# Fused decoder step: the block sums of the first MLP matrix formed in DRAM by copies on SyncE's queue and adding transfers on GpSimd's, beside the z and gate stages, in place of VectorE additions in the MLP

## The chip, the cores and the metric

The kernel runs on one core of a Trainium2 chip. Its engines each work through their own list of instructions in order: TensorE (PE, with weight loads shown apart as PEld), VectorE (DVE), ScalarE (ACT), GpSimd (POOL) and SyncE (SP). Transfers are issued by SP and POOL (and a few by ACT) and are carried by 16 DMA engines. Engines wait for each other, and for transfers, by semaphores.

The metric is the device time of one execution, in microseconds. Lower is better.

## The reference

One step of one layer over 576 tokens: 512 of a new sequence and 8 times 8 of running ones. An RWKV-7 branch and a differential attention branch read the same normalised input, are merged by gates, and a squared-ReLU MLP and a last norm follow. In one line each, in float32:

```python
xn = rmsnorm(x, g_mix);  P = xn @ w_in                      # 1024 x 5376
Pr = P[..., :RWKV_COLS];  Pr = Pr + (Pprev - Pr) * mu_shift # token shift, "z" columns
o_a, S = rwkv7_branch(Pr, S0, lp)                           # per-token state recurrence
o_b = rmsnorm(attend(q, k, v, lam), subln_g) * (1.0 - lam_init)
m = gate_a * (o_a @ w_br_a) + gate_b * (o_b @ w_br_b)       # gates: sigmoid of P's last 2048 columns
x = x + m @ w_out
hn = rmsnorm(x, g_ffn)
x = x + jnp.square(jax.nn.relu(hn @ w_up)) @ w_down         # 1024 x 4096, 4096 x 1024
y = rmsnorm(x, g_final)
```

The states, the new keys and values and the last normalised row are outputs too.

## The kernel before

**Precision.** A float32 product is formed from halves: each operand is written as hi + lo in the fast fp32r format, and three matmuls (hi x hi, hi x lo, lo x hi) make one product. A weight tile therefore costs ACT one instruction (hi, a copy into fp32r) and DVE one (lo, the rest).

**Weights.** `load` brings a row of a weight matrix (128 output columns by all inputs) in pieces of 4 x 128 rows, 256 KB each, over SP's queue into a ring named raw with three buffers. `stream` splits the pieces and yields once per matmul, so that its matmuls can be dealt out between other work; `dense` runs one to its end.

**Stages.** (1) q, k and v and the attention, to about 180 us. Beside it and the next stage run the streams that fill PE's idle time: `shifted`, fourteen rows of the z columns, and then sixteen rows of gates. (2) Four RWKV chains, one per pair of heads (`rwkv` and `chain`), to about 505 us, with the w_brb products as further filler. In each of them `rwkv` normalises the keys: the column sums pn come from PE, POOL raises them to the power -1/2 (nr, line 760) and spreads them over 64 columns (nb, line 763), and PE transposes nb (pk, line 76). POOL also clears state tiles (ST, line 818, and TT, lines 923 and 924), multiplies masks (vm), and stores results of the attention and the chains to DRAM (ob_d, out_Sp, out_Ss). `rpow` puts the same power on POOL for the group norms (var, line 243). (3) w_bra and w_out, to about 604 us. (4) The MLP, and (5) the last norm.

**The MLP.** `up_pair` forms two rows of 128 hidden columns at once by Strassen's scheme in Winograd's form: with the weights cut in four blocks A11, A12, A21, A22 (two rows of columns by two halves of the inputs) and the tokens in two halves, seven products of 12 matmuls replace eight. Four of the seven left operands are sums of blocks:

S1 = A21 + A22, S2 = S1 - A11, S3 = A11 - A21, S4 = A12 - S2.

The tokens' counterparts (t1 to t4) are made once, while w_out is evaluated. A pair loads its two rows of w_up, 512 KB each (line 1188), into a ring of three; DVE forms S1 to S4 in four additions of 128 x 512 (lines 1204, 1205, 1209, 1210, all issued by the helper at line 61); then each operand is split in hi and lo. There are sixteen pairs. `down` multiplies by w_down between the pairs.

**What sets the order.** Instructions are put in order ahead of time by a scheduler that goes by priorities. Loads have FEED plus 1000 times the number of their job, so they go out in the order of their use, as soon as a buffer of the ring is free; filler matmuls have FILL plus the same. `issue_after` says that something is not to be ordered ahead of a given instruction.

Of the kernel before, what the change touches and what calls it, by code (L numbers as in the profile page):

```python
# [8 lines left out]
F32 = mybir.dt.float32  # L9
F32R = mybir.dt.float32r  # L10
I32 = mybir.dt.int32
AF = mybir.ActivationFunctionType
# [3 lines left out]
P = 128  # L16
# [3 lines left out]
NB = 8  # L20
# [5 lines left out]
DFF = 4096  # L26
# [15 lines left out]
def tile_hybrid_step(ctx, tc, xT, xsT, ktab, vtab, s0T, ptab, w_in, vecs, w2a2, g2, lamv,  # L42
                     w_bra, w_brb, w_out, w_up, w_down, cst, bias_p, bias_s,
                     yT, kTo, vTo, Sp, Ss, sh):
    nc = tc.nc
# [9 lines left out]
    ring = {"job": 0}  # L55

    def act(out, in_, func=AF.Copy, **kw):
        ring["act"] = AE.activation(out=out, in_=in_, func=func, **kw)  # L58

    def tt(out, a, b, op, eng=None):  # L60
        ins = (eng or VE).tensor_tensor(out=out, in0=a, in1=b, op=op)  # L61
# [50 lines left out]
    c = const.tile([P, C_END], F32, name="cst_sb")  # L112
# [29 lines left out]
    def load(src, kt, name):  # L142

        job = ring["job"] = ring["job"] + 1
        n = min(kt, ring["piece"])
        raws = []
        with prio(FEED + 1000 * job):
            for k0 in range(0, kt, n):
                raw = ring["pool"].tile([P, n, P], F32, tag="raw", name=f"raw_{name}_{k0}", bufs=3)
                ring["dma"] = nc.sync.dma_start(out=raw, in_=src[:, k0:k0 + n])  # L150
                raws.append(raw)
        return job, raws

    def stream(src, kt, xh, xl, spans, evac, name, raws=None, together=False, banks=None,
# [108 lines left out]
    oa_d = tc.dram_tile([HB, P, NT], F32, name="oa_d")  # L263
    ob_d = tc.dram_tile([HB, P, NT], F32, name="ob_d")
    gt_d = tc.dram_tile([2 * KT, P, NT], F32, name="gt_d")

    zp = pool("zp", stack=ph1)
    zw = pool("zw", 2, stack=ph1)
# [2 lines left out]
    with tc.tile_pool(name="xin", bufs=2, reuse_waits="tile") as xin:  # L271
# [470 lines left out]
    def rwkv(hp):  # L742
# [3 lines left out]
        r, k, vv = Pt[hp], Pt[4 + hp], Pt[8 + hp]  # L746

        def tmp(tag, bufs=1):
            return rt.tile([P, NT], F32, tag="T", name=f"{tag}_{hp}", bufs=6)


        sq = tmp("sq")
        act(sq, k, AF.Square, scale=v(V_KK + hp))
# [101 lines left out]
            act(KBt[:, c0:c0 + cn].rearrange("p c a t -> p (c a t)"), pK[:, :cn * P])  # L855


        s0 = rt.tile([P, NB, 64], F32, tag="s0", name=f"s0_{hp}")
        nc.sync.dma_start(out=s0, in_=s0T[hp])
        (fill if hp == 3 else take)(8)  # L860
        pI = bank(f"pI{hp}")
        for b in range(NB):
# [265 lines left out]
    for i, d in enumerate((0, 4, 1, 5, 2, 6, 3, 7)):  # L1128
        xr = wt_.tile([P, NT], F32, tag="xr", name=f"xr{d}")
        with prio(FEED + 1000 * (ring["job"] + 1) - 1):  # L1130
            nc.sync.dma_start(out=xr, in_=xT[:, d])
        hf = hfs[d] = wt_.tile([P, NT], F32, tag="hf", name=f"hf{d}", bufs=3)
        k = d % 4

        def ev(ps, t0, n, d=d, k=k, xr=xr, hf=hf):
            x, h = ya[:, d, t0:t0 + n], hf[:, t0:t0 + n]
            tt(x, ps, xr[:, t0:t0 + n], ADD)
            act(h, x, scale=v(V_GF + d))
            if d < 4:
                if t0 == 0:  # L1140
                    put("b11", k, h)
                else:
                    t1 = wt_.tile([P, 288], F32, tag="t", name=f"t1_{k}", bufs=4)
                    tt(t1, h, hf[:, :288], SUB)
                    hfs["t1", k] = t1
                    put("t1", k, t1)
            elif t0:
                for n, x, y in (("t2", h, hfs["t1", k]), ("t3", h, hfs[k][:, 288:])):
                    t = hfs[n] = wt_.tile([P, 288], F32, tag="t", name=f"{n}_{k}", bufs=4)
                    tt(t, x, y, SUB)  # L1150
                    put(n, k, t)
                put("b22", k, h)
            else:
                put("b21", k, h)
                t4 = wt_.tile([P, 288], F32, tag="t", name=f"t4_{k}", bufs=4)
                tt(t4, h, hfs["t2"], SUB)
                put("t4", k, t4)
        dense(w_out[d], KT, mh, ml, HALF[::1 if d < 4 else -1], ev, f"wo{d}")

        for j, (t0, n) in enumerate(HALF):  # L1160
            o = acc[:, t0:t0 + n]
            if i == 0:
# [17 lines left out]
    def up_pair(f1):  # L1180
# [2 lines left out]
        for f in (f1, f2):  # L1183
            qs[f] = hq_pool.tile([P, 2, NT], F32R, tag="q", name=f"q{f}")
        with prio(FEED + 1000 * (ring["job"] + 1)):
            rows = [sp_.tile([P, 2, 4, P], F32, tag="raw", name=f"a{f}", bufs=3) for f in (f1, f2)]
            for r, f in zip(rows, (f1, f2)):
                nc.sync.dma_start(out=r.rearrange("p i k w -> p (i k) w"), in_=w_up[f])
        (a11, a12), (a21, a22) = ([r[:, i] for i in range(2)] for r in rows)
        s12, s34 = (sp_.tile([P, 2, 4, P], F32, tag="s", name=f"s{i}_{f1}", bufs=2) for i in (12, 34))  # L1190

        def halve(x, two, after):

            pl = sp_ if two else ring["pool"]
            shape = [P, 2, 4, P] if two else [P, 4, P]
            hi, lo = (pl.tile(shape, F32R, tag=t + "2" * two, name=f"{t}{after}_{f1}", bufs=3)
                      for t in ("hi", "lo"))
            with prio(FEED + 1000 * (ring["job"] + after) + 100):
                act(hi, x)
                tt(lo, x, f32(hi), SUB)  # L1200
            return [(hi[:, i], lo[:, i]) for i in range(2)] if two else (hi, lo)

        with prio(FEED + 1000 * (ring["job"] + 1) + 90):
            tt(s12[:, 0], a21, a22, ADD)
            tt(s12[:, 1], s12[:, 0], a11, SUB)
        S1, S2 = halve(s12, True, 1)
        A11, A12 = halve(rows[0], True, 2)
# [297 lines left out]
```

## Time and profile before

| | us |
|---|---|
| time, median of 2 (999.0 to 1000.22) | 999.61 |
| profiled execution, span | 1004.0 |
| PE busy | 975.5 |
| DVE busy | 689.5 |
| ACT busy | 497.3 |
| POOL busy | 88.3 |

The profiled execution is one run under the profiler, 4.4 us longer than the median of the runs without it. Its times count from the start of its span. Busy time of an engine is the sum over its instructions; a matmul's end is modelled, so a busy PE is not PE at its peak. In a group's row, the number behind the last bar is the idle time of the engine just before the group's instructions, and what ended it. A wait's row names the waiting engine and tile, the releaser, and the time in all, how often, and the longest. The clock in a row of a stretch is the mean clock granted to TensorE, 1.00 being full speed.

### The profile page before, as it was taken

How to read it: one execution, taken by the hardware profiler on the slowest of the kernel's cores; microseconds unless marked ns; L12 is line 12 of the kernel's file. 1: busy time of each engine (PE TensorE's matmuls, PEld its weight loads, DVE VectorE, ACT ScalarE, POOL GpSimd, SP SyncE). 2: the span in 40 equal slices, each digit the busy share in tenths (PEclk: the TensorE clock that was granted, in tenths of full speed). 3: DMA queues.
4: the chain of work that ended last, by engine and by line, in shares of the span. 5: the costliest groups of instructions: out<-in, count | busy, mean ns of one | idle time of the engine just before them, and what ended most of it. 6: DMA issues, size and time to landing. Idle time of an engine off the chain costs nothing.

```text
span 1004.0 us, 24422 instructions
## 1 busy us (share of the span) xinstructions
PE 975.5 (97%) x10012; PEld 919.9 (92%) x10012; DVE 689.5 (69%) x1459; ACT 497.3 (50%) x1094; POOL 88.3 (9%) x171
## 2 busy tenths in 40 slices
PE   8999999899999999999999999999999999999996
PEld 8999998898887878888889999999999999999996
DVE  6698666774946669445588798966666666666744
ACT  6576555354435344443344666644444444444732
POOL 2511001301010340000300000000000000000001
PEclk9999999999989989999999999999999999999998
DMA  7312673121111225222377642222222222221402
GB/s 265 142 66 88 204 221 120 54 64 45 43 47 57 69 87 171 80 70 102 106 215 237 195 152 74 95 85 95 85 85 95 84 85 85 85 84 44 128 10 95
DMA packets 50833, 105.75 MB, mean 105 GB/s; under 512 B 6066, under 2 KB 8114, under 8 KB 50594
## 3 DMA queue, kind: packets, MB, share of 16 engines
q1 hardware_dynamic: 47442, 96.95, 30.2%
q0 software_dynamic: 1648, 5.35, 1.4%
q8 instruction: 79, 1.29, 0.5%
q10 hardware_dynamic: 1632, 1.89, 0.5%
q14 instruction: 32, 0.26, 0.1%
HBM read 89.38 MB, written 14.78 MB: 104 GB/s over the span
## 4 chain that ended last, share of the span: by engine, by line
PE 86%; DVE 6%; ACT 3%; DMA 2%; issue 2%; POOL 1%; SPq 0%; DVEq 0%; POOLq 0%; ACTq 0%
PE ps_dn L72 21%; PE ps_g L72 9%; PE ps_z L72 8%; PE ua L1224 5%; PE ux L1224 5%; PE ps_wo L72 4%; PE uc L1224 3%; PE ud L1224 3%; PE ub L1224 3%; PE ps_k L72 2%; PE ps_brb L72 2%; PE pch L72 2%; PE ps_q L72 2%; PE ps_v L72 2%; PE pA L72 2%
## 5 line engine op out<-in xcount | busy, mean ns | idle before, releaser
L72 PE MATMUL ps_dn<-q,hi_dn 128*128 128x288 f32 x768 | 154.7, 296 | 0.0
L72 PEld LDWEIGHTS ps_dn<-q,hi_dn 128*128 128x128 f32 x768 | 122.8, 188 | 1.5
L72 PE MATMUL ps_dn<-q,lo_dn 128*128 128x288 f32 x384 | 113.2, 295 | 0.0
L72 PE MATMUL ps_g<-xl,hi_g 128*128 128x288 f32 x256 | 80.2, 313 | 0.0
L72 PE MATMUL ps_g<-xh,lo_g 128*128 128x288 f32 x256 | 79.3, 310 | 0.0
L72 PE MATMUL ps_g<-xh,hi_g 128*128 128x288 f32 x256 | 79.2, 310 | 0.0
L72 PEld LDWEIGHTS ps_dn<-q,lo_dn 128*128 128x128 f32 x384 | 72.1, 188 | 0.0
L72 PE MATMUL ps_z<-xh,lo_z 128*128 128x288 f32 (+1 forms) x224 | 69.6, 311 | 0.0
L72 PE MATMUL ps_z<-xh,hi_z 128*128 128x288 f32 (+1 forms) x224 | 68.3, 305 | 0.0
L72 PE MATMUL ps_z<-xl,hi_z 128*128 128x288 f32 (+1 forms) x224 | 67.6, 302 | 0.0
L61 DVE TENSOR_TENSOR ya<-ya,ps_dn 128x288 f32<-128x288 f32 x96 | 43.4, 453 | 29.3 <-PE ps_dn L72 29.3
L58 ACT ACTIVATE hi_dn<-raw_dn 128x512 fp32r<-128x512 f32 x48 | 30.1, 628 | 57.0 <-PE ps_dn L72 57.0
L1224 PE MATMUL ua<-h_b,hi 128*128 128x288 f32 x256 | 53.2, 298 | 0.0
L1224 PE MATMUL ux<-h_t,hi 128*128 128x288 f32 x256 | 52.3, 296 | 0.0
L58 ACT ACTIVATE c<-c 128x288 f32<-128x288 f32 x112 | 48.4, 439 | 7.5 <-DVE c L61 5.8
L72 PEld LDWEIGHTS ps_g<-xh,hi_g 128*128 128x128 f32 x256 | 49.0, 191 | 2.9 <-issue 1.6
L72 PEld LDWEIGHTS ps_g<-xl,hi_g 128*128 128x128 f32 x256 | 49.0, 191 | 1.9
L72 PEld LDWEIGHTS ps_g<-xh,lo_g 128*128 128x128 f32 x256 | 49.1, 192 | 1.4
L58 ACT ACTIVATE hi<-a 128x1024 fp32r<-128x1024 f32 (+1 forms) x32 | 27.1, 846 | 42.0 <-PE ps_dn L72 34.3
L72 PE MATMUL ps_dn<-q,w 128*128 128x320 f32 (+1 forms) x336 | 46.4, 298 | 0.0
L61 DVE TENSOR_TENSOR lo<-s,hi 128x1024 fp32r<-128x1024 f32 x32 | 39.2, 1225 | 10.2 <-ACT hi L58 10.0
L72 PEld LDWEIGHTS ps_dn<-q,w 128*128 128x128 f32 x336 | 45.3, 190 | 0.1
(395 smaller groups left out, 2801.7 us busy)
## 6 DMA issues: line engine op xcount, KB each, us to landing
a<-in_w_up_dram SPq DMA_DIRECT2D x32, 512.0 KB, 3.3
raw_dn<-in_w_down_dram SPq DMA_DIRECT2D x64, 256.0 KB, 2.9
raw_g<-in_w_in_dram SPq DMA_DIRECT2D x32, 256.0 KB, 3.2
raw_z<-in_w_in_dram SPq DMA_DIRECT2D x28, 256.0 KB, 3.0
gt_d<-gg SPq DMA_DIRECT2D x16, 288.0 KB, 2.5
g<-gt_d SPq DMA_DIRECT2D x16, 288.0 KB, 3.7
kp<-in_ktab_dram SPq DMA_DIRECT2D x16, 256.0 KB, 4.0
vp<-in_vtab_dram SPq DMA_DIRECT2D x16, 256.0 KB, 3.7
```

What stands on the lines that cost most here:

```text
L58: ring["act"] = AE.activation(out=out, in_=in_, func=func, **kw)
L61: ins = (eng or VE).tensor_tensor(out=out, in0=a, in1=b, op=op)
L72: ring["mm"] = PE.matmul(out=out, lhsT=lhsT, rhs=rhs, start=start, stop=stop)
L1224: ring["mm"] = PE.matmul(out=ps[:, :288], lhsT=l[:, k], rhs=hb[blk][:, h, k], start=start and i == 0, stop=i == 11, skip_group_check=skip)
```

## The change

The sums S1 to S4 are no longer made by DVE in the MLP. They are made in DRAM, in a new tensor us_d (16 pairs x 128 partitions x 4 sums x 512), while the z and gate streams run:

- Each sum is one copy of a 256 KB block from w_up to us_d, and one adding transfer, which adds another block to what lies there. The copies are issued by SP; the adding transfers by POOL. There are 64 of each, four per pair.
- `block_sums` is a generator that makes one copy at each step. `load` advances it behind each weight piece of the jobs from the thirteenth on, from the first z row, so a copy stands behind each of the first 64 pieces.
- An adding transfer is put into POOL's order six copies after its own copy, and waits for the landing of that newest copy (`sync_after`). The last six come behind the last copies.
- The second and the fourth sum of a pair add the first and the second, which lie in us_d, so their adding transfer waits for the landing of the one before.

Only additions are used, so two of the sums come out with the other sign: us_d holds A21 + A22, A11 + A21 + A22, A11 + A21 and A12 + A11 + A21 + A22, for the second row taken as negative. t1, t2 and t4 change sign to match, and the second row's ReLU has a scale of -1. `up_pair` now loads S1 and S2 (512 KB), the first row (512 KB), S3 and S4 (512 KB) and A22 (256 KB); the three large tiles share a ring of five, where there had been one of three for the rows and one of two for the sums. In `rwkv` the load of the state s0 stands earlier in the code.

```diff
@@ load
                 ring["dma"] = nc.sync.dma_start(out=raw, in_=src[:, k0:k0 + n])
                 raws.append(raw)
+                if job > 12:
+                    with tc.issue_after(ring["dma"].ins):
+                        next(sums_, None)
@@ new
+    us_d = tc.dram_tile([DFF // 256, P, 4, 4 * P], F32, name="us_d")
+    def sync_after(dma, dep):
+        tc.add_manual_dep(dma.ins, dep.ins.name, mybir.DependencyInfo(
+            mybir.DependencyClass.Sync, mybir.DependencyReason.DATA), reason="pace")
+    def block_sums(n, lag):
+        blk = w_up.rearrange("(g o) p (i k) w -> o i p g (k w)", o=2, i=2)
+        dst = us_d.rearrange("g p s c -> s p g c")
+        a11, a12, a21, a22 = (blk[o, i] for o in range(2) for i in range(2))
+        late = []
+        for g in range(0, DFF // 256, n):
+            at = slice(g, g + n)
+            moves = [(s, src, add) for s, src, add in (
+                (0, a21, a22), (2, a11, a21), (1, a11, dst[0]), (3, a12, dst[1]))]
+            for s, src, add in moves:
+                copy = nc.sync.dma_start(out=dst[s][:, at], in_=src[:, at])
+                late.append((s, add, at))
+                if len(late) > lag:
+                    s, add, at_ = late.pop(0)
+                    with prio(FEED):
+                        dma = nc.gpsimd.dma_start(out=dst[s][:, at_], in_=add[:, at_], accum_op=ADD)
+                    sync_after(dma, copy)
+                yield
+        for s, add, at_ in late:
+            with prio(FEED):
+                nc.gpsimd.dma_start(out=dst[s][:, at_], in_=add[:, at_], accum_op=ADD)
+            yield
+    sums_ = block_sums(1, 6)
...
@@ tokens' blocks
-                    tt(t1, h, hf[:, :288], SUB)
+                    tt(t1, hf[:, :288], h, SUB)
...
+                    if n == "t2":
+                        stt(t, h, -1.0, hfs["t1", k], MUL, SUB)
...
-                tt(t4, h, hfs["t2"], SUB)
+                stt(t4, hfs["t2"], -1.0, h, MUL, SUB)
@@ up_pair
-            rows = [sp_.tile([P, 2, 4, P], F32, tag="raw", name=f"a{f}", bufs=3) for f in (f1, f2)]
-            for r, f in zip(rows, (f1, f2)):
-                nc.sync.dma_start(out=r.rearrange("p i k w -> p (i k) w"), in_=w_up[f])
-        (a11, a12), (a21, a22) = ([r[:, i] for i in range(2)] for r in rows)
-        s12, s34 = (sp_.tile([P, 2, 4, P], F32, tag="s", name=f"s{i}_{f1}", bufs=2) for i in (12, 34))
+            s12, a1, s34 = (sp_.tile([P, 2, 4, P], F32, tag="raw", name=f"{n}{f1}", bufs=5)
+                            for n in ("s12", "a1", "s34"))
+            a22 = ring["pool"].tile([P, 4, P], F32, tag="raw", name=f"a22{f1}", bufs=3)
+            flat = lambda t: t.rearrange("p i k w -> p (i k w)")
+            nc.sync.dma_start(out=flat(s12), in_=us_d[f1 // 2, :, 0:2].rearrange("p s c -> p (s c)"))
+            nc.sync.dma_start(out=a1.rearrange("p i k w -> p (i k) w"), in_=w_up[f1])
+            nc.sync.dma_start(out=flat(s34), in_=us_d[f1 // 2, :, 2:4].rearrange("p s c -> p (s c)"))
+            nc.sync.dma_start(out=a22, in_=w_up[f2][:, 4:8])
...
-        with prio(FEED + 1000 * (ring["job"] + 1) + 90):
-            tt(s12[:, 0], a21, a22, ADD)
-            tt(s12[:, 1], s12[:, 0], a11, SUB)
-        with prio(FEED + 1000 * (ring["job"] + 3) + 90):
-            tt(s34[:, 0], a11, a21, SUB)
-            tt(s34[:, 1], a12, s12[:, 1], SUB)
...
-            act(r, c, AF.Relu)
+            act(r, c, AF.Relu, scale=-1.0 if f == f2 else 1.0)
```

The order on the engines, at the three places the prediction turns on. First POOL, from the last store of the sample attention (ob_d) to nb of the first RWKV chain; before:

```order
L243 TENSOR_TENSOR rss<-rss,mhalf 128x2
L426 MEMSET Z_2946 128x1
L711 DMA ob_d<-obs 128x4x64
L818 MEMSET ST_0_2814 64x1152
L818 MEMSET ST_0_2820 64x1152
L760 TENSOR_TENSOR nr_2749<-nr_2749,mhalf 128x10
```

and after, with line numbers of the changed kernel (291 is the adding transfer):

```order
L246 TENSOR_TENSOR rss<-rss,mhalf 128x2
L460 MEMSET Z_2965 128x1
L291 DMA us_d<-in_w_up_dram 128x512
L745 DMA ob_d<-obs 128x4x64
L291 DMA us_d<-in_w_up_dram 128x512
L855 MEMSET ST_0_2835 64x1152
L855 MEMSET ST_0_2841 64x1152
L797 TENSOR_TENSOR nr_2770<-nr_2770,mhalf 128x10
```

Two adding transfers, the ninth and the tenth, have come in: one ahead of the store, one between the store and the memsets that stand in front of nr.

Second POOL, at the end of the chains, from the store of an RWKV output (oa_d) to the group norm's power (var); before:

```order
L980 DMA oa_d<-oa_6714 128x576
L1037 DMA out_Sp_dram<-So_7000 128x64
L1037 DMA out_Sp_dram<-So_7003 128x64
L61 TENSOR_TENSOR vm_7397<-SVU_5282,cst_sb 128x512
L61 TENSOR_TENSOR vm_7399<-SVU_5282,cst_sb 128x512
L61 TENSOR_TENSOR vm_7407<-SVU_5282,cst_sb 128x512
L243 TENSOR_TENSOR var_7422<-var_7422,mhalf 128x9
```

and after, where line 296 is an adding transfer of the last six:

```order
L1015 DMA oa_d<-oa_6817 128x576
L291 DMA us_d<-us_d 128x512
L296 DMA us_d<-in_w_up_dram 128x512
L291 DMA us_d<-us_d 128x512
L296 DMA us_d<-in_w_up_dram 128x512
L291 DMA us_d<-in_w_up_dram 128x512
L296 DMA us_d<-us_d 128x512 x2
L291 DMA us_d<-in_w_up_dram 128x512
L296 DMA us_d<-us_d 128x512 x2
L1072 DMA out_Sp_dram<-So_7103 128x64
L1072 DMA out_Sp_dram<-So_7106 128x64
L61 TENSOR_TENSOR vm_7520<-SVU_5363,cst_sb 128x512
```

Ten adding transfers stand ahead of the out_Sp stores, six of them reading us_d as their second operand behind the group's earlier ones.

Third SP, around the load of the states s0; before:

```order
L150 DMA raw_z_0_3020<-in_w_in_dram 128x512
L150 DMA raw_z_4_3022<-in_w_in_dram 128x512
L859 DMA s_0_2891<-in_s0T_dram 128x512
L859 DMA s_1_3905<-in_s0T_dram 128x512
L150 DMA raw_z_0_3092<-in_w_in_dram 128x512
```

and after (286 is the copy):

```order
L150 DMA raw_z_0_3043<-in_w_in_dram 128x512
L286 DMA us_d<-in_w_up_dram 128x512
L150 DMA raw_z_4_3047<-in_w_in_dram 128x512
L286 DMA us_d<-in_w_up_dram 128x512
L786 DMA s_0_2752<-in_s0T_dram 128x512
L786 DMA s_1_3769<-in_s0T_dram 128x512
L150 DMA raw_z_0_3119<-in_w_in_dram 128x512
```

A copy has come in behind each weight piece; the state loads stand at the same place between the pieces.

More of the change, by code (lines that the diff above doesn't have):

```diff
@@ L749, in tmp @@
             return rt.tile([P, NT], F32, tag="T", name=f"{tag}_{hp}", bufs=6)
+        s0 = rt.tile([P, NB, 64], F32, tag="s0", name=f"s0_{hp}")
+        nc.sync.dma_start(out=s0, in_=s0T[hp])
         sq = tmp("sq")
@@ L855, in rwkv @@
             act(KBt[:, c0:c0 + cn].rearrange("p c a t -> p (c a t)"), pK[:, :cn * P])
-        s0 = rt.tile([P, NB, 64], F32, tag="s0", name=f"s0_{hp}")
-        nc.sync.dma_start(out=s0, in_=s0T[hp])
         (fill if hp == 3 else take)(8)
@@ L1147, in ev @@
             elif t0:
-                for n, x, y in (("t2", h, hfs["t1", k]), ("t3", h, hfs[k][:, 288:])):
+                for n in ("t2", "t3"):
                     t = hfs[n] = wt_.tile([P, 288], F32, tag="t", name=f"{n}_{k}", bufs=4)
-                    tt(t, x, y, SUB)
+                    if n == "t2":
+                        stt(t, h, -1.0, hfs["t1", k], MUL, SUB)
+                    else:
+                        tt(t, h, hfs[k][:, 288:], SUB)
                     put(n, k, t)
@@ L1201, in halve @@
             return [(hi[:, i], lo[:, i]) for i in range(2)] if two else (hi, lo)
-        with prio(FEED + 1000 * (ring["job"] + 1) + 90):
-            tt(s12[:, 0], a21, a22, ADD)
-            tt(s12[:, 1], s12[:, 0], a11, SUB)
         S1, S2 = halve(s12, True, 1)
-        A11, A12 = halve(rows[0], True, 2)
-        with prio(FEED + 1000 * (ring["job"] + 3) + 90):
-            tt(s34[:, 0], a11, a21, SUB)
-            tt(s34[:, 1], a12, s12[:, 1], SUB)
+        A11, A12 = halve(a1, True, 2)
         S3, S4 = halve(s34, True, 5)
```

## The prediction

> **What bounds the kernel now.** I read the page's busy times first, then its chain shares, then busy time by stage, and only then the waits, because a share over the whole span says nothing about which stage a removed instruction stood in.
>
> ```profile
> PE 975.5 (97%) x10012; PEld 919.9 (92%) x10012; DVE 689.5 (69%) x1459; ACT 497.3 (50%) x1094; POOL 88.3 (9%) x171
> PE 86%; DVE 6%; ACT 3%; DMA 2%; issue 2%; POOL 1%; SPq 0%; DVEq 0%; POOLq 0%; ACTq 0%
> ```
>
> TensorE (PE) is busy 97% of the 1004.0 us span and carries 86% of the chain that ended last. By stretch, in us from the span's start (length, then busy time and count of PE, weight load, DVE, ACT, POOL; granted clock; DMA share; GB/s):
>
> ```profile
> core 0: us, PE busy (x) PEld busy (x) DVE busy (x) ACT busy (x) POOL busy (x), PEclk, DMA share, GB/s
> 100.00:150.00 50.00, 48.94 (x554) 46.01 (x554) 31.64 (x88) 27.31 (x73) 2.93 (x6) 1.00 0.68 214
> 182.00:186.00 4.00, 4.00 (x21) 4.00 (x20) 3.11 (x7) 1.61 (x3) 3.69 (x9) 0.57 0.00 0
> 550.00:600.00 50.00, 49.21 (x367) 48.52 (x367) 43.76 (x96) 33.20 (x72) 0.00 (x0) 1.00 0.54 169
> 600.00:960.00 360.00, 360.00 (x2677) 357.48 (x2676) 252.74 (x460) 184.47 (x360) 0.00 (x0) 1.00 0.27 86
> ```
>
> The last row is the MLP without its end: PE is busy for all of 360.00 us at the full granted clock, while DVE is busy for 252.74. Nothing PE waits for can end sooner there, because it waits for nothing. The only sizeable wait that this change can touch is in another stage. These are PE's waits, in us, times and longest:
>
> ```profile
> PE pk L76 <- POOL nb L763: 2.7, 1, 2.7
> PE ps_wo L72 <- DVE ya L61: 0.5, 1, 0.5
> PE ps_wo L72 <- DVE lo_wo L61: 0.2, 1, 0.2
> ```
>
> **Part 1: the sums leave DVE.** Four groups of sixteen tensor_tensor go:
>
> ```profile
> L61 DVE TENSOR_TENSOR s<-a 128x512 f32<-128x512 f32 x16 | 11.0, 688 | 0.3 <-DMA a<-in_w_up_dram 0.3
> L61 DVE TENSOR_TENSOR s<-s,a 128x512 f32<-128x512 f32 x16 | 10.9, 684 | 0.0
> L61 DVE TENSOR_TENSOR s<-a,s 128x512 f32<-128x512 f32 x16 | 10.9, 684 | 0.0
> L61 DVE TENSOR_TENSOR s<-a,a 128x512 f32<-128x512 f32 x16 | 10.9, 683 | 0.0
> ```
>
> That is 11.0 + 3 x 10.9 = 43.7 us of DVE time, 64 instructions. Nearly all of it stands beside a PE without a gap, so it is worth nothing in time. The exception is the first pairs' sums, in 550 to 600, where PE idles 50.00 - 49.21 = 0.79 us; its two waits on DVE above, 0.5 and 0.2, are of that size, and one of the sums (s<-a) waited 0.3 for its row with DVE's queue behind it. A gain there lies between 0 and 0.8; I take -0.3. The sign changes keep instruction counts (t2 and t4 become scalar_tensor_tensor on the same 128x288, Relu gets a scale): nothing, with DVE's 30% of idle time in the MLP as cover.
>
> **Part 2: the MLP's loads.** A pair now loads 1.75 MB (512 + 512 + 512 + 256 KB) instead of 1.0. Sixteen times 0.75 MB is 12.6 million bytes; over 360 us that is some 35 GB/s on top of 86, and at the measured 0.27 for 86 the DMA share becomes about 0.38. In 550 to 600, 0.54 becomes perhaps 0.7. Hidden, as long as a load is issued well ahead. The shared ring is five deep for three tiles a pair, where it was three deep for two, so loads for the next pair still go out before this pair's are consumed. If that cover were missing, each of 16 pairs would wait for part of a landing:
>
> ```profile
> a<-in_w_up_dram SPq DMA_DIRECT2D x32, 512.0 KB, 3.3
> raw_z<-in_w_in_dram SPq DMA_DIRECT2D x28, 256.0 KB, 3.0
> g<-gt_d SPq DMA_DIRECT2D x16, 288.0 KB, 3.7
> out_Ss_dram<-s POOLq DMA_DIRECT2D x4, 256.0 KB, 3.9
> ```
>
> At 3.3 us that is at most 53 us, a price I hold for out of reach, because a pair's seven products and the down products between pairs keep PE for 7 x 1.60 and 12.89 us in the chain that ended last:
>
> ```profile
> 702.32 1.60 PE uc L1224 x12
> 713.52 12.89 PE ps_dn L72 x96
> ```
>
> **Part 3: 64 copies on SP, 64 adding transfers on POOL.** Copies follow weight loads 0 to 63. These are SP's rows of the first load with a copy, of the two around the state load, and of the last ones:
>
> ```profile
> 97.23 1.54 SPq L150 DMA_DIRECT2D raw_z<-in_w_in_dram  x2
> 170.37 2.54 SPq L150 DMA_DIRECT2D raw_z<-in_w_in_dram  x2
> 172.97 0.90 SPq L859 DMA_DIRECT2D s<-in_s0T_dram  x2
> 468.42 0.33 SPq L150 DMA_DIRECT2D raw_g<-in_w_in_dram  x1
> 474.64 11.79 SPq L150 DMA_DIRECT2D raw_brb<-in_w_brb_dram  x2
> ```
>
> On SP an issue is 0.33 us, so 64 more are 21 us over 377 us: SP waits far longer for free buffers. The state load slides behind two copies, by about 1 us and two transfers; its tile is first read over 30 us later, in the first of these matmuls (min, median and longest ns, first and last start): nothing.
>
> ```profile
> L72 PE MATMUL pI<-ST,s x96: 197/206/227, 207.0 to 366.2; 64*64 64x16 f32 x96
> ```
>
> DMA is the dearer side. In 100 to 150 the share is already 0.68 at 214 GB/s, so the full rate is near 214 / 0.68 = 315 GB/s. Twelve of the copies and six adds fall there. Counting an add as one to two copies, that is 18 to 24 times 0.262 MB, 4.7 to 6.3 MB, or 94 to 126 GB/s: 308 to 340 in all. So the stretch comes to its limit; the excess is 0 to (340 - 315) / 315 x 50 = 4 us. Loads run several us ahead of use there, so I take +0.5 and keep 0 to 4.
>
> No trace here shows an adding transfer. The Trainium skill, "Collectives: The Full Stack", section "The bandwidth ceiling: the fold count and why AG ≠ RS ≠ AR", says that a reducing transfer runs at half a copy's rate because each chunk needs two source reads; no run here shows it yet, and by it the upper end, 4 us, would stand in place of 0.5 if no load had slack.
>
> **Part 4: POOL's queue.** An add waits on POOL for the copy six loads later, and whatever stands behind it waits too. One such place is on PE's path, POOL's work before nb of the first RWKV chain:
>
> ```profile
> 175.45 0.80 POOL L711 DMA_DIRECT2D ob_d<-obs  x1 [1.34 <-DVE nr L69]
> 176.29 2.16 POOL L818 MEMSET ST<- 64x1152 f32 x2
> 178.43 2.18 POOL L760 TENSOR_TENSOR nr<-nr,mhalf 128x10 f32<-128x10 f32 x1
> 180.85 0.71 POOL L763 COPY nb<-nr 128x640 f32<-128x640 f32 x1
> 181.61 0.66 PE L76 MATMUL pk<-cst_sb,nb 128*128 128x128 f32 x4 [2.67 <-POOL nb L763]
> ```
>
> These run back to back from 175.45 and PE starts the moment nb is done, so a delay goes to PE one for one. After the change an add (the tenth) stands between ob_d<-obs and the memsets. It waits for the copy behind the load issued at about 172.6 (the second of the two at 170.37, whose 2.54 us end at 172.91). The copy is issued 0.7 later, 173.3. If it lands after L us, the add goes out at 173.3 + L, takes about 0.6, and the memsets start then instead of at 176.29: they are late by L - 2.4. The nearest row is g<-gt_d, a read of a DRAM tile written before: L = 3.7 gives **+1.3**. The raw_z row, 3.0, gives 0.6; the out_Ss row, 3.9, gives 1.5; with the DMA engines crowded L = 5 gives 2.6. Below nothing it cannot go. The half-clock stretch that follows (0.57 in 182 to 186) may last longer, at half its length: up to 1.7 more.
>
> An add's own issue I price by POOL's other transfers:
>
> ```profile
> L588 POOL DMA_DIRECT2D ob_d<-obh x4 | 2.4, 604 | 13.9 <-ACT obh L58 8.7 <-ACT osT L58 5.2
> L711 POOL DMA_DIRECT2D ob_d<-obs x1 | 0.8, 797 | 1.3 <-DVE nr L69 1.3
> ```
>
> These 604 and 797 ns were taken while DVE was busy about two thirds of the time. The Trainium skill, "SBUF — State Buffer", section "SBUF: two separate sides", warns that a transfer issued from GpSimd waits for its descriptors while DVE runs a two-port operation, some 620 ns growing to 3100; no row here shows such a growth, and by it this place would cost 1.3 + 2.5 = 3.8 us.
>
> At the other chains nb has slack; the last is
>
> ```profile
> 370.82 0.72 POOL L763 COPY nb<-nr 128x640 f32<-128x640 f32 x1
> 375.19 0.60 PE L76 MATMUL pk<-cst_sb,nb 128*128 128x128 f32 x4
> ```
>
> with 375.19 - 371.54 = 3.6 us to spare. The memsets of the last TT slide behind seven adds, which at 5.9 us from load to load (377 / 64) is some 41 us; the cover is the 69 us from 376.41 to 445.62:
>
> ```profile
> 376.41 0.33 POOL L924 MEMSET TT<- 32x288 f32 x1
> 445.62 0.33 PE L72 MATMUL pch<-R,TT 64*64 64x64 f32 x4
> ```
>
> At the end of the queue stand the last adds, in front of POOL's work for the last two chains:
>
> ```profile
> 487.19 1.06 POOL L1037 DMA_DIRECT2D out_Sp_dram<-So  x2 [29.93 <-DVE So L69]
> 489.23 3.36 POOL L61 TENSOR_TENSOR vm<-SVU,cst_sb 128x512 f32<-128x512 f32 x3 [0.98 <-DVE SVU L1015]
> 495.86 2.27 POOL L243 TENSOR_TENSOR var<-var,mhalf 128x9 f32<-128x9 f32 x1 [3.27 <-DVE var L69]
> ```
>
> The load at 468.42 has its copy landed by 468.4 + 0.8 + 3.7 = 472.9; then come three adds of one group, each of the last two waiting for the landing of the one before, with about 0.6 for each issue. With A for an add's landing the last of the queue's adds is out near 472.9 + 4 x 0.6 + 2A = 475.3 + 2A. At A = 4.5 (g<-gt_d's 3.7 and once more the time of 256 KB at 315 GB/s, 0.8) that is 484.3, ahead of 487.19. Two out_Sp issues (1.1 us) and vm's 3.4 behind it, it takes A over 6.4 to delay vm and about 8 to delay var: **0** here.
>
> **The sum.** -0.3 + 0 + 0.5 + 1.3 = +1.5 us on a span of 1004.0. Without the profiler the kernel took 999.61 in the median (999.0 to 1000.22), 4.4 below the span; the difference carries over: 999.61 + 1.5, rounded up for a longer half-clock stretch, **1001.5 us**.
>
> **Rivals.** *The adds cannot keep pace (slower).* In each group of four the s1 add waits for the s0 add's landing and the s3 add for the s1 add's, and POOL is in order: a group takes 2A + 3 x 0.6. Loads come 377 us / 64 = 5.9 us apart, 23.6 per four. From A = 10.9 the queue falls behind, and everything POOL does for the RWKV chains with it: 16 x (2A + 1.8 - 23.6), which is 10 us at 11.2 and 35 us at 12, or 1035. Against it: every landing of 256 KB above is 3.0 to 3.9, and crossing 2% (+20 us) needs about 11.5, three times that. For it: no adding transfer has been seen. Chance 0.06.
>
> *DMA is starved in 100 to 150 or A lies at 6 to 10 (slower, within 2%).* 4 us from the excess, or 2 to 6 from late nb, vm and var: 1004 to 1010. For it the 0.68; against it, that loads lead their use. Chance 0.18.
>
> *The gaps fall better (slightly faster).* The copy lands within 2.4 us, DVE's release brings the whole 0.8, and one half-clock stretch of about 3.4 us is not entered, worth 1.7: 999.6 - 2.5 = 997. For it, that the stretch shown follows a gap of only 2.67 us; against it, the same gap, which this change does nothing to close. Chance 0.16.
>
> *DVE paced the MLP after all (faster).* Then 43.7 us would come back: 956. The 360.00 of 360.00 speaks against it. Chance 0.01.
>
> **How the numbers follow.** The forecast, 1000 to 1003.5, has the remaining 0.59. The range 997 to 1010 leaves out the first and last rival and the ends of the others, somewhat under 2 in 10. Within 2% (19.99 us, 979.6 to 1019.6, about what a measurement here can tell from no change) lie all but the first and last rival: faster 0.01, slower 0.06, same 0.93.
>
> **What would show it.** Right: in the changed kernel's rows DVE's busy time falls by about 44 us, 600 to 960 stays at PE 360.00, and PE's wait pk <- POOL nb grows from 2.7 to about 4. The adds' landing decides the main rival: under 6 us it is out, over 11 it rules and POOL's idle time in front of nr is ended by DMA rather than DVE. Wrong: PE waits in the MLP for DMA s or a22, PE gaps in 100 to 150 ended by DMA kp or raw, or a changed count of half-clock stretches that outweighs 1.3 us.

## The result and the profile after

The changed kernel takes 1041.11 us (1041.05 to 1041.17, two runs) against 999.61: 1.0413 times the time before, with a 95% interval of 1.0383 to 1.0443. It is slower by 4.1%, and the range of the prediction ended at 1010. A second measurement (e11, below) gives 1.0386. The profiled execution spans 1039.4 us, 35.4 more than the profiled execution before; the medians differ by 41.5.

The page of the changed kernel: busy times, then the two data queues (packets, MB, share of the 16 DMA engines; q1 carries the transfers that SP issues, q0 those of POOL), then landings (KB each, us from issue to landing).

```profile
PE 986.0 (95%) x10012; PEld 929.2 (89%) x10012; DVE 654.0 (63%) x1395; ACT 497.3 (48%) x1094; POOL 141.0 (14%) x235
...
q1 hardware_dynamic: 61266, 126.32, 37.3%
q0 software_dynamic: 10864, 22.13, 14.1%
...
us_d<-in_w_up_dram SPq DMA_DIRECT2D x64, 256.0 KB, 5.1
...
us_d<-in_w_up_dram POOLq DMA_DIRECT2D x32, 256.0 KB, 7.4
us_d<-us_d POOLq DMA_DIRECT2D x32, 256.0 KB, 5.3
```

DVE gave up what was meant to go: 64 instructions and 689.5 - 654.0 = 35.5 us of busy time. PE runs the same 10012 matmuls and is busy 986.0 instead of 975.5 us. It idles 1039.4 - 986.0 = 53.4 us, where it idled 1004.0 - 975.5 = 28.5. So the 35.4 us are 24.9 of PE's idle time and 10.5 of the same matmuls taking longer.

Where in the program? The busy times by stretch of the changed kernel (columns as in the prediction):

```profile
core 0: us, PE busy (x) PEld busy (x) DVE busy (x) ACT busy (x) POOL busy (x), PEclk, DMA share, GB/s
100.00:150.00 50.00, 48.94 (x555) 46.01 (x554) 31.91 (x88) 26.99 (x73) 5.78 (x10) 1.00 0.90 280
180.00:250.00 70.00, 59.57 (x840) 55.89 (x840) 43.32 (x87) 23.16 (x45) 22.49 (x39) 0.90 0.74 147
250.00:350.00 100.00, 91.06 (x1457) 79.28 (x1442) 59.20 (x133) 44.21 (x100) 16.09 (x21) 0.93 0.54 114
350.00:480.00 130.00, 115.35 (x1998) 101.91 (x1997) 74.48 (x154) 50.13 (x119) 35.23 (x50) 0.93 0.66 158
640.00:1000.00 360.00, 360.00 (x2673) 357.41 (x2672) 219.31 (x397) 182.73 (x354) 0.00 (x0) 1.00 0.35 115
```

and of the kernel before, for the stretches that the prediction did not show:

```profile
180.00:250.00 70.00, 66.90 (x1038) 62.32 (x1039) 45.87 (x95) 29.65 (x59) 10.48 (x28) 0.98 0.18 54
250.00:350.00 100.00, 96.91 (x1449) 84.22 (x1448) 68.48 (x159) 42.78 (x102) 11.11 (x12) 0.97 0.17 54
350.00:480.00 130.00, 126.24 (x2155) 109.59 (x2153) 79.66 (x176) 59.70 (x146) 13.02 (x26) 0.97 0.31 99
```

100 to 150, the one stretch whose DMA load the prediction priced, lost nothing: PE is busy 48.94 of 50 us in both, at a DMA share of 0.90. The MLP lost nothing either. The loss lies in 180 to 480, in the RWKV chains, where DMA had stood at 0.17 to 0.31: PE's idle time is 10.4 + 8.9 + 14.7 = 34.0 us, where it was 3.1 + 3.1 + 3.8 = 10.0. That is 24.0 of the 24.9. The granted clock drops in the same rows. The traces record only full and half clock: half for 44 us in these stretches, in eight pieces, and before for 17 us in three. This is where the matmuls became longer.

What PE waited for in the changed kernel (us, times, longest), first the changed kernel's rows:

```profile
PE pZ L72 <- issue: 11.1, 5, 4.7
PE pk L76 <- POOL nb L800: 6.6, 1, 6.6
PE pW L72 <- issue: 4.5, 2, 2.9
PE pA L72 <- DVE ST L61: 2.8, 1, 2.8
PE pI L72 <- DMA s<-in_s0T_dram: 2.4, 1, 2.4
PE pto L76 <- DVE ot L69: 1.7, 1, 1.7
PE pWc L72 <- issue: 1.5, 1, 1.5
...
PE ps_g L72 <- issue: 1.0, 1, 1.0
```

then those of before:

```profile
PE pZ L72 <- issue: 1.8, 3, 0.8
PE pI L72 <- DMA s<-in_s0T_dram: 1.0, 1, 1.0
PE pW L72 <- issue: 0.5, 1, 0.5
```

The largest growth has no releaser: "issue" went from 1.8 + 0.5 = 2.3 to 11.1 + 4.5 + 1.5 + 1.0 = 18.1 us. The wait for nb grew by 6.6 - 2.7 = 3.9, the one on ST came with 2.8 and the one on ot with 1.7, and the state load added 1.4.

**What "issue" is here.** PE's timeline (start, us, count, idle time before) at one such place, in the changed kernel:

```profile
306.21 0.60 PE L72 MATMUL pZ<-W,Y 32*32 32x32 f32 x47
311.20 0.47 PE L72 MATMUL pZ<-W,Y 32*32 32x32 f32 x17 [4.39 <-issue]
```

and at the same place of the program before:

```profile
292.52 0.60 PE L72 MATMUL pZ<-W,Y 32*32 32x32 f32 x47
293.94 0.34 PE L72 MATMUL pZ<-W,Y 32*32 32x32 f32 x17 [0.82 <-issue]
```

64 independent 32-column products of one group stop after the forty-seventh, in both kernels, with nothing to wait for: their inputs are the same tiles. It is the same instruction at which the stream breaks off, 0.82 us long before and 4.39 after. What arrives in the break is told by the queue of instruction packets. In the changed kernel, from 308.9 to 310.2, it has one packet (queue: packets, MB, share):

```profile
q8 instruction: 1, 0.02, 4.5%
```

and none from 306.9 to 308.9. PE goes on 1.0 us after this window. All eight of the breaks over 0.4 us end 1.2 to 1.5 us after such a packet of 16 KB, and so do the four of before (about 1.4 each). The trace shows more. PE has some 20205 instructions, and this queue brings 79 packets, so a packet holds 256. Numbered in their order, the instructions in front of which PE breaks off leave the same remainder, 193, on division by 256: all nine of the changed kernel's "issue" breaks, all four of before, and those of e1, e2, e4, e6 and e10 below. Each break lies where one packet's instructions end, and PE goes on once the next packet is there. So PE had run out of instructions.

The packets are not slower. In 180 to 480 one takes 1.06 us in the mean, and 1.12 before. They start later: in the median 1.7 us after PE has entered the last packet that it has, where it was 0.8, and at the latest 6.0 us, where it was 2.4. In the chains PE uses up 64 small matmuls and 64 weight loads in some 0.75 us, and packets come as close as 3.4 us there; in the MLP, with matmuls of 288 columns, it uses one up in about 17 us. The Trainium skill, "Runtime: NRT & Kernel Launch", section "Instruction fetch mechanics", describes instructions streamed in 16 KiB blocks over a DMA queue while the current block runs, with a cost that is mostly hidden. The 16 KB packets and the MLP agree; in the chains the fetch is not hidden, and with the new transfers beside it still less.

### The profile page after: what moved, and what is told of

The parts are those of the page before. It is cut to its first block, busy times and chain, and to the rows that moved or that the text cites. A ratio compares the mean times of both kernels' runs of the same rounds, so it can differ in the third digit from the quotient of the medians.

```text
span 1039.4 us, 24673 instructions
## 1 busy us (share of the span) xinstructions
PE 986.0 (95%) x10012; PEld 929.2 (89%) x10012; DVE 654.0 (63%) x1395; ACT 497.3 (48%) x1094; POOL 141.0 (14%) x235
## 3 DMA queue, kind: packets, MB, share of 16 engines
q0 software_dynamic: 10864, 22.13, 14.1%
## 4 chain that ended last, share of the span: by engine, by line
PE 80%; DVE 6%; DMA 4%; issue 4%; ACT 4%; POOL 2%; SPq 0%; DVEq 0%; POOLq 0%; ACTq 0%
PE ps_dn L72 20%; PE ps_g L72 8%; PE ps_z L72 7%; PE ua L1259 5%; PE ux L1259 5%; PE ps_wo L72 3%; PE ps_k L72 3%; PE uc L1259 3%; PE ud L1259 2%; PE ub L1259 2%; PE ps_q L72 2%; DMA us_d<-in_w_up_dram 2%; PE ps_brb L72 2%; PE pch L72 2%; PE ps_v L72 2%
```

## Experiments

Times are medians, ratios are to the kernel before, measured beside each on the same chip (medians of 1001.2 to 1002.5).

**e1: the copies alone.** SP's 64 copies stay, all adds go.

```diff
-                    with prio(FEED):
-                        dma = nc.gpsimd.dma_start(out=dst[s][:, at_], in_=add[:, at_], accum_op=ADD)
-                    sync_after(dma, copy)
```

> The 64 copies on SP and the MLP's new loads stay; the 64 adding transfers on POOL are left out, so us_d holds single blocks and not sums. Theory 1 (PE's instructions are fetched late, because the copies and adds fill the DMA engines in the RWKV stage): a part of the loss stays with the copies. Of the 2048-byte packets in the trace after, a copy's take about 0.1 us and an add's 0.25, so copies are some 0.3 of the added DMA time: 1005 to 1014, waits of pZ, pW and pWc on 'issue' 3 to 7 us instead of 17. Theory 2 (POOL's in-order waits for landings delay nb and the cleared tiles): nothing waits on POOL any more, 999 to 1002, and pk <- nb is back at 2.7.

1010.28 us, 1.0097 [1.0062, 1.0132]. Copies that no add waits for cost about 10 us, a quarter of the loss. The nb wait is the old one. The waits for ST (2.3) and for the state load (2.0) are nearly those of the changed kernel, so they come with the copies alone; "issue" is 4.1 us in all.

**e2: POOL's transfers without the adding.** The order, the waits and the number of transfers are those of the changed kernel; each copies where it added.

```diff
-                        dma = nc.gpsimd.dma_start(out=dst[s][:, at_], in_=add[:, at_], accum_op=ADD)
+                        dma = nc.gpsimd.dma_start(out=dst[s][:, at_], in_=add[:, at_])
```

> As after, order and waits the same, but each of POOL's 64 transfers is a plain copy instead of an adding one (us_d holds single blocks). Theory 1: DMA time falls from about 0.35 to 0.2 us per pair of packets, so 1010 to 1025, the 'issue' waits halve. Theory 2: POOL still waits for every landing, but landings are shorter (about 5 instead of 7 us): 1025 to 1038.

1026.45 us, 1.0248 [1.0207, 1.0289]. The adding itself is worth about 1.5% (4.1, or 3.9 in e11, less 2.5), the rest comes without it.

**e3: the MLP's new loads alone.** No copy and no add; the MLP loads as many bytes, from rows of the matrix.

```diff
-                if job > 12:
-                    with tc.issue_after(ring["dma"].ins):
-                        next(sums_, None)
...
-            nc.sync.dma_start(out=flat(s12), in_=us_d[f1 // 2, :, 0:2].rearrange("p s c -> p (s c)"))
+            nc.sync.dma_start(out=s12.rearrange("p i k w -> p (i k) w"), in_=w_up[f2])
```

> No copies and no adds; the MLP takes its 1.75 MB per pair and has no additions on DVE, but S1 to S4 are read as plain rows of w_up. Both theories: the MLP side of the change is worth nothing or a little, 998.5 to 1001, PE busy for all of 600 to 960.

1002.62 us, 0.9999 [0.9982, 1.0016]. The sums are left out, so this is the whole benefit of the change without its price: from 600 to 960 us DVE is busy 221.66 us instead of 252.74, PE is busy for 360.00 as before, and the time is that of before. There was nothing to gain.

**e4: all 128 transfers and waits, a sixteenth of the bytes.** Each moves 32 of 512 columns.

```diff
-                copy = nc.sync.dma_start(out=dst[s][:, at], in_=src[:, at])
+                copy = nc.sync.dma_start(out=dst[s][:, at, :32], in_=src[:, at, :32])
...
-                        dma = nc.gpsimd.dma_start(out=dst[s][:, at_], in_=add[:, at_], accum_op=ADD)
+                        dma = nc.gpsimd.dma_start(out=dst[s][:, at_, :32], in_=add[:, at_, :32], accum_op=ADD)
```

> 64 copies and 64 adding transfers with the same order, waits and queues as after, but each moves only 32 of 512 columns (16 KB); the MLP reads plain rows of w_up in place of the sums. Theory 1: no traffic, no late fetches: 999 to 1004. Theory 2: POOL waits as often, with landings of 3 to 5 us: 1020 to 1035, pk <- nb above 5 us.

1005.84 us, 1.005 [1.0032, 1.0068]. Instructions, queues and waits cost 5 us, the bytes the other 35. PE's wait for nb:

```profile
PE pk L76 <- POOL nb L800: 3.8, 1, 3.8
```

It is up by 1.1. That is near the prediction's +1.3, but by luck: POOL's row of the ninth add shows no wait for a landing.

```profile
175.27 0.89 POOL L291 DMA_DIRECT2D us_d<-in_w_up_dram  x1 [0.40 <-issue]
```

Here it is the issuing of two adds that pushes the memsets back. "issue" of PE is 3.1 in all, near its old size, although POOL and SP issue as often as in the changed kernel and move as many packets.

**e6: the same bytes copied, all on SP.** Two plain copies per weight piece, none on POOL.

```diff
-                    with prio(FEED):
-                        dma = nc.gpsimd.dma_start(out=dst[s][:, at_], in_=add[:, at_], accum_op=ADD)
-                    sync_after(dma, copy)
+                    nc.sync.dma_start(out=us_e.rearrange("g p s c -> s p g c")[s][:, at_], in_=src[:, at_])
```

> Behind each of the 64 pieces two plain copies on SP (the second into a DRAM tensor that nothing reads), nothing on POOL; us_d holds single blocks, not sums. It has the bytes of the run with plain copies on POOL, without POOL's waits. Theory 1: traffic alone costs twice what one copy per piece costs (8.5 above before), so 1016 to 1022, some 5 below the run with POOL's waits; pk <- nb stays at 2.7. If POOL's waits had made that run's second half of the loss: 1010.

1019.64 us, 1.0184 [1.0168, 1.0199]: about twice e1's loss. POOL issues none of its copies, and PE's waits show it:

```profile
PE pZ L72 <- issue: 4.9, 4, 2.3
PE pW L72 <- issue: 4.5, 2, 3.4
...
PE pk L76 <- POOL nb L798: 2.7, 1, 2.7
PE ps_g L72 <- issue: 2.5, 1, 2.5
```

The nb wait is the old 2.7, and "issue" is 11.9. So the breaks need neither POOL nor the adding, only transfers beside the chains. e2 moves the same bytes and has POOL's waits besides (nb 5.0): the 0.7 points between the two are about what those cost.

The engine time of the transfers orders these kernels, roughly. From the share of q1 times the span, less that of e3 (33.6% of 1002.6), and the share of q0, less that of before, for e1, e2 and e6 (44.8% of 1019.0 in e6; the rows of e1, then of e2):

```profile
q1 hardware_dynamic: 61266, 126.32, 39.1%
```

```profile
q1 hardware_dynamic: 61266, 126.32, 38.6%
q0 software_dynamic: 6768, 22.13, 7.8%
```

e1's 64 copies hold all 16 engines for 0.391 x 1007.2 - 0.336 x 1002.6 = 57 us, 0.89 each. e6's 128 hold them for 120. In e2, 59 and, at 1.4% before, 0.078 x 1025.5 - 0.014 x 1004.0 = 66, together 125. In the changed kernel 51 and 0.141 x 1039.4 - 14.1 = 132, together 183. In e4, by shares of 34.4% and 3.7% of 1003.2, it is 8 and 23.

| kernel | engine time added, us | "issue" of PE, us | time lost |
|---|---|---|---|
| e3, no copies or adds | 0 | 2.9 | 0.0% |
| e4, same count, a sixteenth of the bytes | 31 | 3.1 | 0.5% |
| e1, copies | 57 | 4.1 | 1.0% |
| e6, two copies on SP | 120 | 11.9 | 1.8% |
| e2, copies on SP and POOL | 125 | 9.8 | 2.5% |
| changed kernel | 183 | 18.1 | 4.1% |

"issue" stands clear of e3's 2.9 only from e6 on; at e1 it explains little of the loss. The scheduler orders each kernel anew, but PE's matmuls stand in e1 and e2 exactly as in the changed kernel, so their order is not what lies between 1.0%, 2.5% and 4.1%. In e4 and e6 they differ from it in 494 and 547 of the 10012 places, all behind 380 us.

**e5: the same work in the MLP.** The copies and adds of pairs 4 to 15 stand behind the pairs' own loads; pairs 0 to 3 take their sums on DVE as before.

```diff
-        for g in range(0, DFF // 256, n):
+        for g in range(4, DFF // 256, n):
...
+                ring["dma"] = nc.sync.dma_start(out=a22, in_=w_up[f2][:, 4:8])
+            with tc.issue_after(ring["dma"].ins):
+                for _ in range(5):
+                    next(sums_, None)
```

> The sums of pairs 4 to 15 are made by the same copies and adding transfers (48 and 48), but issued behind the first pairs' loads in the MLP instead of behind z and gate pieces; pairs 0 to 3 keep their sums on DVE. Theory 1 (late instruction fetches): in the MLP PE takes two instructions per 134 ns and fetches 16 KB every 17 us, so the same traffic delays nothing: 999 to 1003. If instead a transfer costs time wherever it lies (DMA engines or DRAM as such, loads that land late): 48/64 of the loss, 1025 to 1035.

1002.82 us, 1.0012 [0.9999, 1.0024]. Three quarters of the transfers, landing later still (a copy 6.0 us, adds 8.9 and 7.6), and a DMA share of 0.66 cost next to nothing here:

```profile
600.00:960.00 360.00, 359.91 (x2672) 357.23 (x2672) 224.05 (x406) 183.93 (x357) 36.16 (x44) 1.00 0.66 171
```

The share itself does no harm. What it stands beside decides: in the MLP PE waits for none of these loads, and instructions are consumed slowly.

**e8 and e10: which part of the early work.** e8 leaves pairs 0 to 4 behind the first 20 weight pieces (97 to 215 us) and moves the rest to the MLP; e10 leaves the first 20 pieces free, puts pairs 0 to 10 behind the next 44 and the rest into the MLP.

```diff
-    sums_ = block_sums(1, 6)
+    sums_ = block_sums(1, 6, 0, 5)
+    more_ = block_sums(1, 6, 5, 16)
...
+            with tc.issue_after(ring["dma"].ins):
+                for _ in range(5):
+                    next(more_, None)
```

(e10 has 0 to 11 and 11 to 16, and starts at `job > 22`.)

> All 64 sums by copies and adding transfers, none on DVE, but none in the span from about 230 to 500 us in which the RWKV chains send PE runs of 32-column matmuls: pairs 0 to 4 behind the first 20 pieces (97 to 215 us), pairs 5 to 15 behind the pairs' own loads in the MLP. Theory 1 (late fetches in the chains): the 'issue' waits stay near 2 us although DMA is over 0.8 busy in 100 to 180; what is left is the late nb before the first chain and its half-clock stretch, 3 to 7 us, so 1003 to 1008. If crowded DMA engines cost time at any instruction rate: 20/64 of the loss or more, 1012 to 1020.

> The complement of the last run: nothing behind the first 20 pieces, pairs 0 to 10 by copies and adds behind pieces 20 to 63 (215 to 500 us, the RWKV chains), pairs 11 to 15 in the MLP. Theory 1, with both kinds of delay adding up: after minus the 18 us that the first 20 pieces cost, 1020 to 1026, 'issue' waits of pZ, pW and pWc of 12 to 18 us and pk <- nb at 2.7. If most of the loss came from late landings in 97 to 215: 1003 to 1010, 'issue' waits below 6.

e8 took 1020.62 us, 1.0192 [1.0167, 1.0217]; e10 took 1032.74 us, 1.0304 [1.0277, 1.0332]. I had forecast 1003 to 1008 and 1020 to 1026: both missed, since I took the "issue" breaks for nearly all of the loss. e8 loses 18 us without them (0.3 us in all). Its longest waits:

```profile
PE pk L76 <- POOL nb L801: 6.8, 1, 6.8
PE ps_z L72 <- ACT hi_z L58: 4.1, 1, 4.1
PE ua L1263 <- DVE acc L61: 2.8, 1, 2.8
```

and e10's:

```profile
PE pZ L72 <- issue: 9.8, 4, 4.8
PE ua L1263 <- DVE acc L61: 3.7, 1, 3.7
```

The wait for hi_z looks like a late raw_z, but POOL's and ACT's rows in front of it say otherwise:

```profile
222.82 0.81 POOL L296 DMA_DIRECT2D us_d<-us_d  x1 [4.40 <-DMA us_d<-us_d]
223.68 0.14 POOL L461 MEMSET Z<- 128x1 f32 x2
223.81 0.78 ACT L58 ACTIVATE tz<-Z,vec 128x585 f32<-128x585 f32 x1 [6.93 <-POOL Z L461]
```

ACT works in order, and in front of hi_z it waits for a Z whose first column POOL clears. That memset stands behind the last adds of the early pairs, which wait for landings one after the other. It is POOL's queue again, as with nb; but this bunch of last adds is e8's own, since in the changed kernel it comes near 500 us.

There are two ways to lose, then, and they lie apart: behind the first 20 pieces, POOL's work held up behind adds that wait for landings (in e10 the wait for nb is the old 2.7); behind the others, late instructions. The two losses, 18 and 31 us, sum to more than the changed kernel's 40, because both kernels also have a burst of transfers at the start of the MLP with a wait of their own (ua, 2.8 and 3.7). Ahead of it they do add up, nearly. The first w_brb product (ps_brb) starts at 446.1 us before, at 455.8 in e8, at 467.2 in e10 and at 480.4 in the changed kernel: 9.7 and 21.1 late, against 34.3 (the 9.7 has the 4.1 of hi_z in it).

**e9: adds without the wait for the copy six loads later.**

```diff
-                    sync_after(dma, copy)
```

> As after, but an adding transfer no longer waits for the copy six loads on, only for what it adds to and what it reads; the traffic is the same, and the adds go out earlier on POOL. Theory 1 (crowded DMA engines delay fetches and landings): nearly the whole loss stays, 1034 to 1044. Theory 2 (the pacing wait holds POOL back): 1005 to 1020.

1054.7 us, 1.0542 [1.0521, 1.0563], slower than with the wait, where I expected 1034 to 1044. PE's two longest waits:

```profile
PE psb L72 <- DMA kp<-in_ktab_dram: 12.3, 2, 12.0
PE pk L76 <- POOL nb L799: 9.3, 1, 9.3
```

A page of the key table (kp) comes 12 us late, which the changed kernel has nowhere. So the wait is not what costs. That the adds, which then go out as early as POOL's queue lets them, are what made this page late is likely, but no run shows it apart.

**e7: copies in another shape.** e6 with each copy written as eight groups of 16 partitions; `by8(ap)` is `ap.rearrange("(a b) g c -> a b (g c)", a=8)`.

```diff
-                copy = nc.sync.dma_start(out=dst[s][:, at], in_=src[:, at])
+                copy = nc.sync.dma_start(out=by8(dst[s][:, at]), in_=by8(src[:, at]))
```

> As the run with two copies on SP per piece, but each copy is written as 8 groups of 16 partitions, in the hope that it is dealt to 8 DMA engines and not to 16. If that takes effect, a copy's landing grows by about 0.8 us. Theory 1 with all fetches on engines that the copies leave free: the 'issue' waits go back to about 2 us and the time to 1004 to 1010. Theory 1 with fetches on the same engines: these are twice as crowded, 1022 to 1035. If the shape takes no effect: 1017 to 1022 as before.

1222.08 us, 1.2192 [1.2171, 1.2212], and inconclusive. The copies land in 4.8 us as e6's do, but the order on the engines is another one (PE's differs in more than a thousand rows), and PE's longest wait, 38.0 us, is for gg of DVE, work that moved with it. It says nothing of the shape.

**e11: the changed kernel again,** beside e9 and e10.

> The changed kernel itself beside the two runs above: 1038 to 1044.

1040.3 us, 1.0386 [1.0355, 1.0418]; "issue" is 17.4 us.

## Why the prediction was wrong

**Part 1 and Part 2 held.** DVE's sums stood beside a PE without a gap; e3 measures both parts together at nothing. 600 to 960 was to stay at 360.00, and the MLP, now from 640 to 1000, did. The DMA share of the MLP came to 0.35 where 0.38 was worked out. Of DVE's 43.7 us only 35.5 left the busy time; the rows of a group add up instructions that overlap their neighbours.

**Part 3 is the step that failed,** at "DMA is the dearer side. In 100 to 150 the share is already 0.68". I priced DMA where it was fullest and only against the full rate: 0 to 4 us. I counted twelve of the 64 copies and six of the adds there; nine and four were issued there. 43 and 44 lie in 180 to 480, where the share had been 0.17 to 0.31, and I priced them at an issue each on SP and POOL. That holds only if a transfer that finds room delays nobody. It was the other way round: the full stretch lost no time, and the half-empty ones lost it, because what stands beside the transfers there is on PE's path. Instruction packets (15.8 us of waits), the state load, the ob loads and the copies that adds wait for all came later. And gaps are paid again: 27 more us at half clock. The price of that step was +0.5; by e1 the copies alone are about +10, and by e4 the bytes of copies and adds are 35 of 40.

The sentence "its tile is first read over 30 us later [...]: nothing" on the state load is wrong too. It holds for the first pair of heads. For the second the load and its reader lie close together, as SP's and PE's rows of the changed kernel show:

```profile
380.83 3.89 SPq L786 DMA_DIRECT2D s<-in_s0T_dram  x2
```

```profile
386.58 1.11 PE L72 MATMUL pI<-ST,s 64*64 64x16 f32 x32 [2.44 <-DMA s<-in_s0T_dram]
```

I took the first start of a group of 96 matmuls for all of them. Another case is the load of ob, 4.6 us before, 7.0 now in the median. In the chain of waits such a load stands for 6.83 us, then ACT's obh, and in the end DVE's ST, for which pA waits 2.8.

**Part 4 had the place and the mechanism right, the size too small.** POOL's rows in front of nb, in the changed kernel:

```profile
180.25 0.89 POOL L291 DMA_DIRECT2D us_d<-in_w_up_dram  x1 [3.68 <-DMA us_d<-in_w_up_dram]
...
182.89 2.16 POOL L855 MEMSET ST<- 64x1152 f32 x2
...
187.24 0.71 POOL L800 COPY nb<-nr 128x640 f32<-128x640 f32 x1
```

The memsets start at 182.89 instead of 176.29. It is the ninth add, in front of the ob_d store, that waits (3.68 us), and not the tenth as I had it. The wait for nb is 6.6 where I said "about 4". The term that was too small is L: SP issues the copy that the ninth add waits for at 173.19, and POOL goes on at 180.25, 7.1 us later, where L was 3.7. Copies issued about then land in 7.0 us in the median. With L = 7.0 the prediction's L - 2.4 gives 4.6; the wait grew by 3.9. e4's 3.8, with copies of 16 KB that land in 3.0, is the price of the adds' issues alone.

Nor was nb the only such place. POOL's power rr, in front of the attention's ot, stands behind an add too:

```profile
167.38 0.81 POOL L291 DMA_DIRECT2D us_d<-us_d  x1 [5.18 <-DMA us_d<-in_w_up_dram]
167.93 1.33 POOL L246 TENSOR_TENSOR rr<-rr,mhalf 128x4 f32<-128x4 f32 x1
```

That is the 1.7 us of PE's wait for ot. The tail of POOL's queue cost nearly what was said: the wait for vm is 0.4.

**The adding transfer.** By the queues' shares an add of 256 KB holds the 16 engines for 132 / 64 = 2.07 us; a plain copy from POOL takes 66 / 64 = 1.03. The ratio is 2.0. The sentence from the Trainium skill, "Collectives: The Full Stack", section "The bandwidth ceiling: the fold count and why AG ≠ RS ≠ AR" (half a copy's rate), agrees; counting "one to two copies" was right, and multiplying it only by the 18 to 24 in 100 to 150 was not. The other warning that was cited, of descriptors held up to 3100 ns (the Trainium skill, "SBUF — State Buffer", section "SBUF: two separate sides"), did not come true: POOL's issue of an add takes 839 ns in the mean, of a plain transfer 536.

**The rivals.** "The adds cannot keep pace" gave 1035, near the time that came, by a mechanism that did not: adds land in 7.4 and 5.3 us, short of the 10.9 from which it decides, and POOL's idle time in front of nr is ended by DVE. "DMA is starved in 100 to 150 or A lies at 6 to 10" had A nearly right and nb's 2 to 6 us right, but no word of the chains. The list of what would make it wrong names "a changed count of half-clock stretches"; it came true as a consequence, not as a cause. No rival held that a quiet stretch has more to lose than a full one, and the 0.93 for no change rested on that.

**What stays open.** That PE runs out of instructions in the "issue" breaks is shown by their places and by the packets; that the bytes beside them delay the packets, by e4 against the changed kernel and by e5, e6, e8 and e10. Why a packet starts later beside them is not shown, and no run changed the fetch alone. How the 35 us divide among instructions, POOL's queue, late loads and the clock is read from waits and places, and not measured part by part. No version beat the kernel before: e5, which makes three quarters of the sums in the MLP, ties with it, and so does e3, which makes none.

## What to carry to other kernels

Before moving work onto idle DMA engines, ask what else uses them in that stretch and how far ahead of its reader it runs: a stage with a share of 0.17 to 0.31 and tight chains idled PE 24 us longer, one at 0.90 lost nothing, and an MLP at 0.66 next to nothing (though e8 and e10 have a wait of 2.8 and 3.7 us at its start). Instruction packets are among those users, so long runs of tiny matmuls are a poor place for bulk transfers. An engine that works in order is another: whatever stands behind a transfer that waits for a landing waits too. And a removed instruction is worth something only where its engine is waited for: 360.00 of 360.00 said that beforehand, and then any price at all makes the change a loss.

## What was unexpected of the hardware

- PE runs dry of instructions in the middle of a group of matmuls. It shows as idle time with "issue" as its releaser, up to 0.8 us at a time before and 4.7 after, always a multiple of 256 instructions after the break before, and the engine goes on 1.2 to 1.5 us after a 16 KB packet of the instruction queue.
- One 256 KB transfer holds the 16 DMA engines for 0.89 us as a copy issued by SP, 1.03 issued by POOL, 2.07 as an add.
- Late landings need no full DMA: with the copies and adds, raw_z lands in 3.9 us instead of 2.8 in 180 to 250, at a share of 0.74, and raw_g in 4.5 instead of 3.2 in 350 to 480, at 0.66. In 250 to 350, at 0.54, raw_g lands in 3.0 as before (2.9), while an instruction packet there started 6.0 us after PE had entered the last that it had.
- Removing the pacing wait made the kernel slower by 1.5 points (1.0542 against 1.0386 in the same batch): here a wait on a queue did more good than harm.
